# Retention outputs turned by VectorE and gated in the last stage, in a hybrid retention and MLA decode step

## The chip, the cores and the metric

The kernel runs on one core of one Trainium2 chip, as one launch. The metric is the device time of that launch in microseconds. A core has TensorE (PE, whose weight loads are shown apart as PEld), VectorE (DVE), ScalarE (ACT), GpSimd (POOL) and SyncE (SP). SP and ACT each have a queue from which they issue DMAs. All five follow their own instruction streams in order and wait for each other by semaphores.

## The reference, cut to what matters

One layer of a decoder mixes 1024 prompt tokens and 8 sequences of 4 sample tokens, 1056 columns in all. One wide projection of the normalised input gives retention queries, keys and values (4 heads, 256 for q and k, 512 for v), a SiLU gate for the retention outputs, the MLA latents and gates, and two merge gates. Retention runs over the prompt in 8 chunks of 128 tokens for each head:

```python
scores = jnp.einsum('bihd,bjhd->bhij', q, k) * dmask[None]
intra = jnp.einsum('bhij,bjhe->bihe', scores, v)
cross = jnp.einsum('bihd,bhde->bihe', q, s_prev) * q_decay[None, :, :, None]
s_new = (jnp.exp(c * log_g)[None, :, None, None] * s_prev
         + jnp.einsum('bjhd,bjhe->bhde', k * k_decay[None, :, :, None], v))
```

The retention output is normalised for each token and head over its 512 features, multiplied by a weight for each feature and by the gate, and only then projected:

```python
def retention_out(o, rg, gn_w):
    mu = jnp.mean(o, axis=-1, keepdims=True)
    var = jnp.mean(jnp.square(o - mu), axis=-1, keepdims=True)
    on = ((o - mu) * lax.rsqrt(var + EPS)).reshape(b, s, RET_VW).astype(rg.dtype)
    return on * gn_w * jax.nn.silu(rg)

h_ret = retention_out(ret_o, rg, ret_gn_w) @ w_down_ret
h_mla = (mla_o * jax.nn.silu(mg)) @ w_down_mla
merged = jax.nn.sigmoid(ga) * h_ret + jax.nn.sigmoid(gb) * h_mla
x = x + merged @ w_out
x = x + jax.nn.sigmoid(x @ w_ple_gate) * (ple @ w_ple_proj)
```

A final RMSNorm gives the outputs. All data are 32-bit floats.

## The kernel before

**Arithmetic.** Nearly every product is made of three matmuls on operands that are split into a high and a low part (`hi`, `lo`, type fp32r): `mac` (L263) multiplies high by high, high by low and low by high. The high part is a copy by ScalarE or GpSimd, the low part a subtraction by VectorE (`lo_of`, L199). `gemm` (L271) makes a 128 x 1056 output in three thirds of 352 columns, each over `nk` blocks of the inner dimension, in one of two PSUM tiles `mm`; an `evac` function takes each third out of PSUM.

**Stages in order of time.** Input turning and latents; gate projections beside the samples' attention over the paged cache, to about 730 us; retention, head by head, about 730 to 1335 us; MLA prompt attention, to about 1632 us; the MLA down projection, to about 1718 us; the retention down projection in two halves of the inner dimension, to about 1890 us; the output projection, to about 2003 us; the embedding gate and the outputs, to the end.

**Order of the work.** The program is traced as Python generators that yield costs; `woven` (L116) takes the next step of the stream that is furthest behind its share. A planner then puts the instructions of each engine in order, allots tiles from pools with a fixed number of buffers, and sets the semaphores. A DMA whose tile isn't free waits on its queue, and what stands behind it on that queue waits too.

**A retention head.** `head_qk` (L823) projects queries and keys with four gemms (q0, q1, k0, k1), each on weights that `load_w` (L254) loads and splits just ahead of it; two raw buffers `wr` and two pairs `wh`, `wl` serve all such weights. `values_of` makes the values of one chunk in `mm`. In `prompt_chunks`, `front` makes the scores of a chunk (L928), masks them (`smr`) and splits them (`smh`, `sml`); it also loads the turned keys (`knl`) that came through DRAM in `kD`. `back` multiplies scores and values into `po`, adds the product with the state, updates the state, and ends with `group_norm`, whose last instruction is ScalarE's `on` (L891). The rest of `back` is run in the next chunk's weave (`due`): `gate_out` (L899) turns `on` with four transposes on TensorE (L904), multiplies each by the feature weight `gnw` and by the gate `g` on VectorE (L908), and stores the product to `goD` (L910). `gate_in` (L894) has loaded `g` from `gtD`, where the gate projections left it, features on the partitions. Tile `g` has three buffers.

**The samples** of a head follow its chunks (`sample_state`). Their 32 tokens stand in eight rows of each group of 32 partitions of `on`; `gate_out` collects them with matmuls against a selecting matrix (L906). For all heads but the last this is put off (`late`) to the start of the next head.

**The last stages.** `gated` (L1465) loads 128 features of `goD`, already gated, for all 1056 columns; `split_gated` splits them to `gh` and `gl`. The pool `w4` has three buffers, which the gates of the merge (`gate`, L1481), the residual's tiles `xT` and two others share. In the last part `sample_rooms` (L1677) and `sample_load` (L1700) prepare the samples' share of the embedding gate: the rooms take one of 23 buffers of pool `x`, and the loads share the two `wr` buffers. They are called after the loop over the first half's four prompt tiles.

Of the kernel before, what the change touches and what calls it, by code (L numbers as in the profile page):

```python
# [162 lines left out]
def decode_step(ctx: ExitStack, tc: tile.TileContext, A: dict, O: dict):  # L163
# [29 lines left out]
    def b32(ap):  # L193
        return ap.bitcast(F32)
# [22 lines left out]
    gaD = [dram.tile([P, NT], F32, tag=f"ga{f}", name=f"ga{f}") for f in range(8)]  # L217
    gbD = [dram.tile([P, NT], F32, tag=f"gb{f}", name=f"gb{f}") for f in range(8)]
    mgD = [dram.tile([P, NT], F32, tag=f"mg{f}", name=f"mg{f}") for f in range(8)]
    gtD, goD = ([dram.tile([P, 4, NT], F32, tag=f"{n}{h}", name=f"{n}{h}") for h in range(HR)] for n in ("gt", "go"))  # L220
    latD = dram.tile([NLAT // 32, 32, SEQ], F32, tag="latD", name="latD")
    xTD = dram.tile([P, 8, NT], F32, tag="xTD", name="xTD")
    pTD = dram.tile([PLE // 32, 32, NT], F32, tag="pTD", name="pTD")
# [30 lines left out]
    def load_w(src, nk):  # L254

        hi, lo = wtiles()
        src = src.rearrange("(k p) f -> p k f", p=P)
        for k in range(0, nk, 4):
            ks = slice(k, min(k + 4, nk))
            stage(src[:, ks], hi[:, ks], lo[:, ks])  # L260
        return hi, lo
# [559 lines left out]
    kD = [dram.tile([SEQ // 32, 32, DK], F32, tag=f"kD{i}", name=f"kD{i}") for i in range(2)]  # L821

    def head_qk(h, X):  # L823
        for name, col in (("q", C_RQ), ("k", C_RK)):
            dst = X[name] = [tok(f"{name}{m}", dt=F32) for m in range(2)]

            def first(j, ps, sl, dst=dst):
                act.copy(dst[0][:, sl], ps)

            def second(j, ps, sl, dst=dst, name=name):  # L830
                x = wst.tile([P, TH], F32, tag="gev", name="rx", bufs=2)
                act.copy(x, ps)
                c, s = cosR[:, sl], sinR[:, sl]
                x0, x1 = dst[0][:, sl], dst[1][:, sl]
                t = [p4.tile([P, TH], F32, tag=f"rt{i}", name=f"rt{i}", bufs=1) for i in range(2)]
                dve.tensor_tensor(out=t[0], in0=x0, in1=s, op=ALU.mult)
                dve.tensor_tensor(out=x1, in0=x, in1=c, op=ALU.mult)
                pool.tensor_tensor(out=x1, in0=x1, in1=t[0], op=ALU.add)
                dve.tensor_tensor(out=t[1], in0=x, in1=s, op=ALU.mult)
                dve.tensor_tensor(out=x0, in0=x0, in1=c, op=ALU.mult)  # L840
                pool.tensor_tensor(out=x0, in0=x0, in1=t[1], op=ALU.subtract)
                if name == "k":
                    n = min(TH, SEQ - j * TH)
                    bs = slice(j * TH // 32, (j * TH + n) // 32)
                    for m in range(2):
                        st = p4.tile([P, TH], F32, tag=f"rt{m}", name="kb", bufs=1)[:, :n].rearrange("p (b r) -> p b r", r=32)
                        dve.transpose(st, dst[m][:, j * TH:j * TH + n].rearrange("p (b r) -> p b r", r=32))
                        for a in range(0, P, 32):
                            sp.dma_start(kD[h % 2][bs, :, m * P + a:m * P + a + 32].rearrange("b i f -> i b f"), st[a:a + 32])
            for m, evac in enumerate((first, second)):  # L850
                w = load_w(w_in[:, col + h * DK + m * P:col + h * DK + (m + 1) * P], 8)
                yield from gemm(w, xn, evac, 8)
            own = X[name + "S"] = p4.tile([P, 2, NR], F32, tag=name + "S", name=name + "S", bufs=2)
            for m in range(2):
                act.copy(own[:, m], dst[m][:, SEQ:])
# [35 lines left out]
        act.activation(on[:n], po, AF.Identity, bias=nb[:n], scale=s[:n])  # L891
        return on

    def gate_in(h, n, cols):  # L894
        g = p4.tile([P, 4, P], F32, tag="g", name="g", bufs=3)[:, :, :n]
        sp.dma_start(g, gtD[h][:, :, cols])
        return g

    def gate_out(h, on, n, cols, g):  # L899
        pt = tr()  # L900
        for f in range(4):
            o = pt[:, f * P:f * P + n]
            if n == P:
                pe.transpose(o, on[:, f * P:(f + 1) * P], ident)  # L904
            else:
                pe.matmul(o, on[:, f * P:(f + 1) * P], C("sel"), start=True, stop=True)  # L906
        for f in range(4):
            dve.scalar_tensor_tensor(out=g[:, f, :], in0=pt[:, f * P:f * P + n], scalar=gnw[:, 4 * h + f:4 * h + f + 1],  # L908
                                     in1=g[:, f, :], op0=ALU.mult, op1=ALU.mult)
        sp.dma_start(goD[h][:, :, cols], g)  # L910

    def pair(name, w, bufs, rows_=P):
        return tuple(p4.tile([rows_, w], F32R, tag=name + s, name=name + s, bufs=bufs) for s in "hl")
# [1 line left out]
    def prompt_chunks(h, X):  # L915
# [30 lines left out]
        def back(c, parts):  # L946
            sl = slice(c * P, (c + 1) * P)
            smh, sml, kh, kl = parts
            vh, vl = V.pop(c)
            if c:  # L950
                qh, ql = pair("qc", DK, 1)
                for m in range(2):
                    ms = slice(m * P, (m + 1) * P)
                    hi_pool(qh[:, ms], q[m][:, sl])
                    lo_of(ql[:, ms], q[m][:, sl], qh[:, ms])
            g = gate_in(h, P, sl)
            po = ac()
            mac(po, (smh, sml), (vh, vl), True, c == 0)
            yield 0.65
            for m in range(2 if c else 0):  # L960
                Sh, Sl = T["S"]
                ms, vs = slice(m * P, (m + 1) * P), slice(m * DV, (m + 1) * DV)
                mac(po, (qh[:, ms], ql[:, ms]), (Sh[:, vs], Sl[:, vs]), False, m == 1)
                yield 0.65
            for m in range(2):
                ms, vs = slice(m * P, (m + 1) * P), slice(m * DV, (m + 1) * DV)
                pS = ac()
                mac(pS, (kh[:, ms], kl[:, ms]), (vh, vl), True, True)
                if c:
                    dve.scalar_tensor_tensor(out=S[:, vs], in0=S[:, vs], scalar=gC, in1=pS, op0=ALU.mult, op1=ALU.add)  # L970
                else:
                    act.copy(S[:, vs], pS)
                yield 0.65
            if c < 7:
                Sh, Sl = T["S"] = tuple(p4.tile([P, 2 * DV], F32R, tag="st", name=f"St{n}", bufs=4) for n in "hl")
                for m in range(2):
                    vs = slice(m * DV, (m + 1) * DV)
                    hi_pool(Sh[:, vs], S[:, vs])
                    lo_of(Sl[:, vs], S[:, vs], Sh[:, vs])
            on = group_norm(po, P, C("qd", h, 1), C("qd2", h, 1))  # L980
            yield None
            gate_out(h, on, P, sl, g)
            yield 0.43

        def ahead(u):

# [6 lines left out]
        yield 1.0  # L993
        yield from values_of(0, X, V)
        while late:
            gate_out(*late.pop())
        due = iter(())
        for c in range(8):
            if c == 7:
                X["st"] = [states(h, 0, 0)]  # L1000
            u = back(c, parts)
            if c < 7:
                parts = front(c + 1)
                yield 1.0
                yield from woven((chain(due, ahead(u)), 3.9), (values_of(c + 1, X, V), 5.5))
                due = u
        yield None
        yield from due
# [17 lines left out]
    def sample_state(h, X):  # L1026

        q, k = X["qS"], X["kS"]
        g4 = float(np.exp(NS * lg[h]))
        sl = slice(SEQ, NT)  # L1030

        def weights(k):
            raw = p4.tile([P, DV], F32, tag="vn" + "hl"[k % 2], name="wvS", bufs=2)
# [53 lines left out]
        yield 2.0  # L1087
        px = ac()
        pe.matmul(px, sm.rearrange("p r x -> p (r x)"), vs, start=True, stop=False, skip_group_check=True)
        g = gate_in(h, NR, sl)  # L1090
        out = O["ret_sample"][0].rearrange("(r i) h (m p) e -> i m h p r e", i=2, m=2)
        turns = [(i, m) for i in range(2) for m in range(2)]
        loaded = X["st"]
# [19 lines left out]
        on = group_norm(px, P, C("qdS", h, 1), C("qd2S", h, 1))  # L1113
        yield 0.3
        if h + 1 < HR:
            late.append((h, on, NR, sl, g))
        else:
            gate_out(h, on, NR, sl, g)
            yield 0.5

    HB = 4

# [341 lines left out]

    def gated(f, pl):  # L1465
        lo = pl("gl")
        sp.dma_start(b32(lo), goD[f // 4][:, f % 4, :])
        return lo

    def split_gated(hi, lo):  # L1470

        for j in range(3):
            sl = slice(j * TH, (j + 1) * TH)
            split(b32(lo)[:, sl], hi[:, sl], lo[:, sl])
        return hi, lo

    def load_gated(f, pl):
        lo = gated(f, pl)
        return split_gated(pl("gh"), lo)

    def gate(src, f):  # L1481
        t = w4("gate", dt=F32)
# [24 lines left out]
    mph.close()  # L1507
    rph = ctx.enter_context(ExitStack())
    xr_ = slots(rph.enter_context(tc.tile_pool(name="x2", bufs=1, side="right")), "x2", 17)
    gx[7] = split_gated(xr_("gh"), gx[7])  # L1510
    merged, nxt = [], []
    for half in range(2):
        for f in range(8):
# [226 lines left out]
    for T in range(4):  # L1740
        if T < 2:
            residual(T + 2)
        proj_products(T, 0)
        joined(T, 0)
        if T < 2:
            gate_products(T + 2, 0)
        if T == 3:
            split_weight(WP, 1, 0, raw_weight("w_ple_proj", 1, 0))
        gate_weight(1, 2 * T, wtiles() if T == 3 else None)
    sp.dma_start(fnw, A["final_norm_w"].unsqueeze(0).to_broadcast([P, D]))  # L1750
    sample_rooms()
    for i in range(2):
        sample_load()
    units = [(T, 1) for T in range(4)] + [(T, H) for T in range(4, 8) for H in range(2)]
    for n, (T, H) in enumerate(units):
        if n == 1:
# [51 lines left out]
```

## Time and profile before

| | before |
|---|---|
| median of 3 runs | 2126.14 us (2125.18 to 2126.87) |
| profiled execution | 2132.47 us, span 2130.7 us |
| PE busy | 2088.9 us, 98% of the span |
| PEld, DVE, ACT, POOL busy | 1805.8, 1241.0, 698.1, 307.6 us |
| DMA | 321.91 MB in 346869 packets, mean 151 GB/s |
| ACT's DMA queue (q10) | 17280 packets, 21.63 MB |
| granted TensorE clock | 0.997 |

The span is the time between the first and the last instruction; the execution's own time is a little longer. The profiled execution is 6.3 us, 0.3%, above the median. Busy time of an engine is the union of its instructions' intervals; TensorE's matmuls overlap one another, so the distance between two starts, not a duration, says what a matmul takes. A line of the timeline has start, length, engine, line of the kernel, operation, tiles as out<-in, shape, count and, in brackets, how long the engine sat idle before it and for whom. A line of the waits has who waited for whom, the total, how often, and the longest. A row of an engine's line (L904 and so on) has the count, the shortest, median and longest duration in ns, and the first and last start in us. A queue is marked with q (ACTq, SPq): there the length is that of the issue, not of the transfer.

### The profile page before, as it was taken

The numbers are of one execution on the slowest core, as the hardware profiler recorded it, in microseconds if no ns is written. First come the engines' busy times: TensorE is split into PE (matmuls) and PEld (weight loads), VectorE is DVE, ScalarE is ACT, GpSimd is POOL, SyncE is SP. The second block draws the span as 40 slices with busy tenths as digits, with TensorE's granted clock in tenths as the row PEclk, the third lists the DMA queues.
The fourth block names the chain that finished last, engine by engine and source line by source line (L and its number), as shares of the span: only waits on it lengthen the run. The fifth ranks groups of instructions, "written<-read, shape, count | busy, mean of one in ns | idle before, by whom it ended". The sixth has DMA issues, their size and how long they took to land. (4 is left out here: it accounts for less than half of the span.)

```text
span 2130.7 us, 38543 instructions
## 1 busy us (share of the span) xinstructions
PE 2088.9 (98%) x15282; PEld 1805.8 (85%) x15282; DVE 1241.0 (58%) x2791; ACT 698.1 (33%) x1455; POOL 307.6 (14%) x517
## 2 busy tenths in 40 slices
PE   8999999999999999999999999999999999999998
PEld 7998777777777897888888887788888999999976
DVE  6524555565655356767676774877777353454433
ACT  6312232333433222322222221454556341232221
POOL 2210111111110022222222220122211000000000
PEclk9999999999999999999999999999999999999999
DMA  7586656566565432654726647210112453236642
GB/s 204 136 245 211 235 202 230 202 237 222 196 238 172 126 76 68 205 161 124 237 73 185 184 134 256 60 49 19 38 52 82 152 174 99 92 119 133 178 145 91
DMA packets 346869, 321.91 MB, mean 151 GB/s; under 512 B 126944, under 2 KB 294048, under 8 KB 342592
## 3 DMA queue, kind: packets, MB, share of 16 engines
q1 hardware_dynamic: 320192, 213.92, 34.4%
q0 software_dynamic: 9216, 83.89, 10.5%
q10 hardware_dynamic: 17280, 21.63, 2.8%
q8 instruction: 120, 1.97, 0.4%
q14 instruction: 61, 0.50, 0.1%
HBM read 246.69 MB, written 72.69 MB: 150 GB/s over the span
## 5 line engine op out<-in xcount | busy, mean ns | idle before, releaser
L267 PE MATMUL mm<-xh,wh 128*128 128x352 f32 x1344 | 456.4, 340 | 2.3 <-POOL wh L197 1.6
L269 PE MATMUL mm<-xh,wl 128*128 128x352 f32 x1344 | 436.3, 325 | 2.1 <-DVE wl L200 2.1
L268 PE MATMUL mm<-xl,wh 128*128 128x352 f32 x1344 | 436.3, 325 | 0.0
L267 PEld LDWEIGHTS mm<-xh,wh 128*128 128x128 f32 x1344 | 253.0, 188 | 86.1 <-issue 74.2
L269 PEld LDWEIGHTS mm<-xh,wl 128*128 128x128 f32 x1344 | 253.9, 189 | 4.0 <-DVE wl L200 2.4
L268 PEld LDWEIGHTS mm<-xl,wh 128*128 128x128 f32 x1344 | 254.0, 189 | 3.2 <-issue 2.1
L688 DVE STREAM_TRANSPOSE kt<-craw 128x512 f32<-128x512 f32 x256 | 161.2, 681 | 109.3 <-PE sc L692 74.8
L200 DVE TENSOR_TENSOR wl<-wr,wh 128x512 fp32r<-128x512 f32 (+2 forms) x203 | 140.1, 703 | 88.8 <-ACT wh L248 56.8
L248 ACT CAST wh<-wr 128x512 fp32r<-128x512 f32 x150 | 89.9, 617 | 203.5 <-PE mm L268 177.4
L440 ACT ACTIVATE gev<-mm 128x352 f32<-128x352 f32 x120 | 55.5, 462 | 229.4 <-PE mm L269 215.6
L267 PE MATMUL mm<-mh,wh 128*128 128x352 f32 x384 | 124.5, 324 | 1.4 <-ACT mh L1186 0.8
L268 PE MATMUL mm<-ml,wh 128*128 128x352 f32 x384 | 124.8, 325 | 0.7 <-DVE ml L200 0.6
L269 PE MATMUL mm<-mh,wl 128*128 128x352 f32 x384 | 124.3, 324 | 0.0
L269 PE MATMUL mm<-gh,wl 128*128 128x352 f32 x384 | 124.3, 324 | 0.0
L267 PE MATMUL mm<-gh,wh 128*128 128x352 f32 x384 | 124.3, 324 | 0.0
L268 PE MATMUL mm<-gl,wh 128*128 128x352 f32 x384 | 124.2, 323 | 0.0
L267 PE MATMUL mm<-wv,xh 128*128 128x512 f32 x256 | 103.5, 404 | 0.0
L268 PE MATMUL mm<-wv,xh 128*128 128x512 f32 x256 | 100.9, 394 | 0.0
L269 PE MATMUL mm<-wv,xl 128*128 128x512 f32 x256 | 100.8, 394 | 0.0
L692 PE MATMUL sc<-kt,q 32*32 32x512 f32 x2560 | 91.2, 600 | 0.0
L891 ACT ACTIVATE on<-ac,gb,gs 128x512 f32<-128x512 f32 x36 | 28.0, 778 | 157.5 <-DVE gb L889 152.4
L267 PEld LDWEIGHTS mm<-mh,wh 128*128 128x128 f32 x384 | 72.4, 188 | 1.9 <-ACT mh L1186 1.0
(419 smaller groups left out, 4370.6 us busy)
## 6 DMA issues: line engine op xcount, KB each, us to landing
wr<-in_w_in_dram SPq DMA_DIRECT2D x144, 256.0 KB
st<-in_state_ret_dram SPq DMA_DIRECT2D x32, 512.0 KB
out_ret_sample_dram<-st SPq DMA_DIRECT2D x32, 512.0 KB
gt<-gev ACTq DMA_DIRECT2D x48, 176.0 KB
gl<-go SPq DMA_DIRECT2D x16, 528.0 KB
gate<-ga SPq DMA_DIRECT2D x16, 528.0 KB
g<-gt SPq DMA_DIRECT2D x32, 256.0 KB
go<-g SPq DMA_DIRECT2D x32, 256.0 KB
```

The source lines that it names most:

```text
L200: dve.tensor_tensor(out=out, in0=src, in1=b32(hi), op=ALU.subtract)
L248: hi_by[0](hi, raw)
L267: pe.matmul(out, wh, xh, start=first, stop=False)
L268: pe.matmul(out, wh, xl, start=False, stop=False)
L269: pe.matmul(out, wl, xh, start=False, stop=last)
L440: act.activation(t, ps, func)
L688: dve.transpose(kt[:, 2 * i + s].rearrange("p (n r) -> p n r", r=32), src)
L692: pe.matmul(sc[32 * v:32 * v + 32, q, :], Q["q4"][qs_, j + v // 2, 2 * (g % 2) + v % 2, :], kt[qs_, v, :], start=n == 0, stop=n == NJ // 2 ...
L891: act.activation(on[:n], po, AF.Identity, bias=nb[:n], scale=s[:n])
```

## The change

Four things are changed.

1. The retention output of a chunk is turned by VectorE in blocks of 32 x 32 into a tile `st` (the `g` buffers), and not by TensorE. The tile is kept in a list, and in the next chunk's turn ScalarE issues four DMAs that store it to `goD`, which is now laid out as 16 blocks of 32 features; each contiguous piece of a store has 32 tokens, 128 B. The samples' `on` goes the same way, with 8 tokens a piece, and the selecting matmuls go.
2. The product with `gnw` and the gate is made in the last stages: `gated` loads 128 ungated features from `goD` and the gate from `gtD`, the latter into a buffer of `w4`, and one instruction of VectorE makes the product of 128 x 1056, which is then split.
3. In `head_qk` the weights of the next gemm are asked for at the fourth step of the gemm before. The weave's total for the chunk's own work is 3.5 in place of 3.9.
4. `sample_rooms` and the first two `sample_load` are called after the second of the four prompt tiles.

```diff
-    gtD, goD = ([dram.tile([P, 4, NT], F32, tag=f"{n}{h}", name=f"{n}{h}") for h in range(HR)] for n in ("gt", "go"))
+    gtD = [dram.tile([P, 4, NT], F32, tag=f"gt{h}", name=f"gt{h}") for h in range(HR)]
+    goD = [dram.tile([DV // 32, 32, NT], F32, tag=f"go{h}", name=f"go{h}") for h in range(HR)]
...
     def head_qk(h, X):
-        for name, col in (("q", C_RQ), ("k", C_RK)):
+        cols = [col + h * DK + m * P for col in (C_RQ, C_RK) for m in range(2)]
+        ws = []
+
+        def ask():
+            if cols:
+                col = cols.pop(0)
+                ws.append(load_w(w_in[:, col:col + P], 8))
+
+        ask()
+        for name in "qk":
...
             for m, evac in enumerate((first, second)):
-                w = load_w(w_in[:, col + h * DK + m * P:col + h * DK + (m + 1) * P], 8)
-                yield from gemm(w, xn, evac, 8)
+                for i, cost in enumerate(gemm(ws.pop(0), xn, evac, 8)):
+                    if i == 3:
+                        ask()
+                    yield cost
...
-    def gate_in(h, n, cols):
-        g = p4.tile([P, 4, P], F32, tag="g", name="g", bufs=3)[:, :, :n]
-        sp.dma_start(g, gtD[h][:, :, cols])
-        return g
-
-    def gate_out(h, on, n, cols, g):
-        pt = tr()
-        for f in range(4):
-            o = pt[:, f * P:f * P + n]
-            if n == P:
-                pe.transpose(o, on[:, f * P:(f + 1) * P], ident)
-            else:
-                pe.matmul(o, on[:, f * P:(f + 1) * P], C("sel"), start=True, stop=True)
-        for f in range(4):
-            dve.scalar_tensor_tensor(out=g[:, f, :], in0=pt[:, f * P:f * P + n], scalar=gnw[:, 4 * h + f:4 * h + f + 1],
-                                     in1=g[:, f, :], op0=ALU.mult, op1=ALU.mult)
-        sp.dma_start(goD[h][:, :, cols], g)
+    turned_out = []
+
+    def turn_out(h, on, n, t0):
+        st = p4.tile([P, DV], F32, tag="g", name="g", bufs=3).rearrange("p (b r) -> p b r", r=32)
+        dve.transpose(st, on.rearrange("p (b r) -> p b r", r=32))
+        turned_out.append((h, st, n, t0))
+
+    def store_out():
+        while turned_out:
+            h, st, n, t0 = turned_out.pop(0)
+            for a in range(4):
+                act.dma_start(goD[h][:, :, t0 + a * n:t0 + a * n + n].rearrange("b i t -> i b t"), st[32 * a:32 * a + 32, :, :n])
...
             on = group_norm(po, P, C("qd", h, 1), C("qd2", h, 1))
             yield None
-            gate_out(h, on, P, sl, g)
-            yield 0.43
+            store_out()
+            turn_out(h, on, 32, c * P)
...
-            gate_out(*late.pop())
+            turn_out(*late.pop())
...
-                yield from woven((chain(due, ahead(u)), 3.9), (values_of(c + 1, X, V), 5.5))
+                yield from woven((chain(due, ahead(u)), 3.5), (values_of(c + 1, X, V), 5.5))
...
         if h + 1 < HR:
-            late.append((h, on, NR, sl, g))
+            late.append((h, on, NS * 2, SEQ))
         else:
-            gate_out(h, on, NR, sl, g)
-            yield 0.5
+            store_out()
+            turn_out(h, on, NS * 2, SEQ)
+            store_out()
...
     def gated(f, pl):
         lo = pl("gl")
-        sp.dma_start(b32(lo), goD[f // 4][:, f % 4, :])
-        return lo
+        sp.dma_start(b32(lo), goD[f // 4][4 * (f % 4):4 * (f % 4) + 4].rearrange("b i t -> (b i) t"))
+        g = w4("rg", dt=F32)
+        sp.dma_start(g, gtD[f // 4][:, f % 4, :])
+        dve.scalar_tensor_tensor(out=g, in0=b32(lo), scalar=gnw[:, f:f + 1], in1=g, op0=ALU.mult, op1=ALU.mult)
+        return lo, g
...
-            split(b32(lo)[:, sl], hi[:, sl], lo[:, sl])
+            split(g[:, sl], hi[:, sl], lo[:, sl])
...
         gate_weight(1, 2 * T, wtiles() if T == 3 else None)
+        if T == 1:
+            sample_rooms()
+            for i in range(2):
+                sample_load()
     sp.dma_start(fnw, A["final_norm_w"].unsqueeze(0).to_broadcast([P, D]))
-    sample_rooms()
-    for i in range(2):
-        sample_load()
```

More of the change, by code (lines that the diff above doesn't have):

```diff
@@ L955, in back @@
                     lo_of(ql[:, ms], q[m][:, sl], qh[:, ms])
-            g = gate_in(h, P, sl)
             po = ac()
@@ L1029, in sample_state @@
         g4 = float(np.exp(NS * lg[h]))
-        sl = slice(SEQ, NT)
         def weights(k):
@@ L1089, in sample_state @@
         pe.matmul(px, sm.rearrange("p r x -> p (r x)"), vs, start=True, stop=False, skip_group_check=True)
-        g = gate_in(h, NR, sl)
         out = O["ret_sample"][0].rearrange("(r i) h (m p) e -> i m h p r e", i=2, m=2)
@@ L1466, in gated, with split_gated @@
         lo = pl("gl")
-        sp.dma_start(b32(lo), goD[f // 4][:, f % 4, :])
-        return lo
-    def split_gated(hi, lo):
+        sp.dma_start(b32(lo), goD[f // 4][4 * (f % 4):4 * (f % 4) + 4].rearrange("b i t -> (b i) t"))
[3 more added lines that the diff above has]
+        return lo, g
+    def split_gated(hi, lo, g):
         for j in range(3):
             sl = slice(j * TH, (j + 1) * TH)
-            split(b32(lo)[:, sl], hi[:, sl], lo[:, sl])
+            split(g[:, sl], hi[:, sl], lo[:, sl])
         return hi, lo
     def load_gated(f, pl):
-        lo = gated(f, pl)
-        return split_gated(pl("gh"), lo)
+        lo, g = gated(f, pl)
+        return split_gated(pl("gh"), lo, g)
     def gate(src, f):
@@ L1509, in decode_step @@
     xr_ = slots(rph.enter_context(tc.tile_pool(name="x2", bufs=1, side="right")), "x2", 17)
-    gx[7] = split_gated(xr_("gh"), gx[7])
+    gx[7] = split_gated(xr_("gh"), *gx[7])
     merged, nxt = [], []
```

## The prediction

> **What bounds the kernel now.** I read the page first, then the table by stretches (the retention chunks of the second head; the MLA down projection; the first half of the retention down projection and what follows), then TensorE's own waits in the retention stage.
>
> ```profile
> PE 2088.9 (98%) x15282; PEld 1805.8 (85%) x15282; DVE 1241.0 (58%) x2791; ACT 698.1 (33%) x1455; POOL 307.6 (14%) x517
> ...
> 926.00:1001.00 75.00, 75.00 (x360) 61.98 (x360) 55.93 (x144) 20.28 (x41) 20.67 (x39) 1.00 0.34 89
> 1632.00:1718.00 86.00, 86.00 (x534) 86.00 (x533) 33.08 (x61) 29.22 (x48) 2.84 (x6) 1.00 0.48 157
> 1718.00:1890.00 172.00, 172.00 (x1066) 172.00 (x1065) 84.77 (x163) 52.07 (x90) 0.00 (x0) 1.00 0.38 119
> ...
> PE ac L269 <- DVE ll L200: 1.1, 1, 1.1
> PE ac L268 <- DVE vnl L200: 1.1, 4, 0.3
> PE ac L267 <- ACT lh L1200: 1.0, 1, 1.0
> PE ac L267 <- ACT vnh L873: 0.6, 1, 0.6
> PE tr L906 <- ACT on L891: 0.4, 1, 0.4
> PE tr L904 <- ACT on L891: 0.4, 1, 0.4
> ```
>
> The columns of the middle lines are stretch, length, busy time of PE, PEld, DVE, ACT, POOL, then granted clock, DMA share and GB/s. TensorE is busy 75 of 75 us at full clock; the six last lines are all its waits between 790 and 1335 us, 4.6 us in all. So a matmul taken away here shortens the run, unless what it covered comes to light. Busy time overlaps, so I price matmuls by distances between starts, in one steady chunk:
>
> ```profile
> L904 PE MATMUL tr<-cst,on x128: 271/273/328, 801.6 to 1284.6; 128*128 128x128 f32 x128
> ...
> 970.66 0.60 PE L928 MATMUL ac<-q,k 128*128 128x128 f32 x4
> 971.10 0.60 PE L904 MATMUL tr<-cst,on 128*128 128x128 f32 x4
> 971.46 0.48 PE L267 MATMUL mm<-wv,xh 128*128 128x512 f32 x1
> ...
> 972.25 0.39 PE L267 MATMUL ac<-vnh,smh 128*128 128x512 f32 x1
> ...
> 980.60 0.60 PE L928 MATMUL ac<-q,k 128*128 128x128 f32 x4
> ...
> 969.58 0.78 ACT L891 ACTIVATE on<-ac,gb,gs 128x512 f32<-128x512 f32 x1 [6.76 <-DVE gb L889]
> 970.91 0.58 ACT L873 CAST vnh<-mm 128x512 fp32r<-128x512 f32 x1 [0.56 <-PE mm L269]
> 971.68 0.30 ACT L932 CAST smh<-smr 128x128 fp32r<-128x128 f32 x1 [0.18 <-DVE smr L931]
> ...
> 971.30 0.29 DVE L931 TENSOR_TENSOR smr<-ac,cst 128x128 f32<-128x128 f32 x1 [0.45 <-PE ac L928]
> 971.53 0.69 DVE L200 TENSOR_TENSOR vnl<-mm,vnh 128x512 fp32r<-128x512 f32 x1
> 973.34 1.12 DVE L908 SCALAR_TENSOR_TENSOR g<-tr,gnw,g 128x128 f32<-128x128 f32 x4
> ```
>
> A chunk lasts 9.94 us (970.66 to 980.60); the four transposes take 971.46 - 971.10 = 0.36 us. ACT is free for 6.76 us in each chunk ahead of `on`.
>
> **The change part by part.**
>
> *Transposes.* L904 has x128 transposes, four for each of 32 chunks: 32 x 0.36 = 11.5 us off TensorE. The samples' selecting matmuls stand below: 1327.30 - 1326.38 = 0.92 us a head. I count three heads, 2.8 us; the fourth is in the tail. With them goes the 0.4 us wait of L904 for `on`.
>
> *What comes to light.* Between the scores and the first product with `smh` TensorE now does the transposes and three value matmuls (971.10 to 972.25); `smh` is ready at 971.98, `vnl` at 972.22. Without the transposes the same order would reach that product at 971.89 and the one with `vnl` at 972.12: 0.1 us short each, one after the other rather than added, so about 0.1 us x 28 = 3 us if the order stays. In the first chunk of a head, where nothing is turned, the order already moves:
>
> ```profile
> 793.36 0.48 PE L267 MATMUL mm<-wv,xh 128*128 128x512 f32 x1
> ...
> 793.91 0.42 PE L267 MATMUL ac<-vnh,smh 128*128 128x512 f32 x1
> ...
> 794.87 0.40 PE L268 MATMUL ac<-vnl,smh 128*128 128x512 f32 x1
> ```
>
> The first product comes between value matmuls and no wait is shown. I take 1 us (0 to 3).
>
> *VectorE.* One 128x512 transpose, 0.67 us by the row below, for four multiplies, 1.12 us (973.34): 0.45 us less a chunk on an engine that is not the bound. It may start in the 0.45 us gap ahead of `smr` and delay `smr` and `vnl` by some 0.2 us; with value matmuls to fill, 0 (0 to 28 x 0.2 = 6 us).
>
> *ScalarE's stores.* Each chunk adds four DMA issues to ACT, and takes a load and a store off SP.
>
> ```profile
> L441 ACTq DMA_DIRECT2D gt<-gev x48: 326/326/327, 374.2 to 652.8; - x48
> L849 SPq DMA_DIRECT2D kD<-kb x96: 302/462/816, 783.0 to 1223.4; - x96
> L910 SPq DMA_DIRECT2D go<-g x36: 519/560/753, 805.4 to 1328.3; - x36
> L688 DVE STREAM_TRANSPOSE kt<-craw x256: 659/670/714, 187.1 to 702.4; 128x512 f32<-128x512 f32 x128
> 731.00 2.19 SPq L896 DMA_DIRECT2D g<-gt  x3
> ```
>
> ACT pays 0.33 us for an issue of 128 pieces; SP 0.46 for the `kD` stores, which have the new store's 128 B pieces, and 0.56 for 512 pieces. The new store has 32 partitions x 16 blocks = 512 pieces, so nearest is 0.56: four make 1.3 to 2.2 us, for 36 groups 47 to 81 us of ACT in a stage where it has 6.76 of 9.94 us free. In that gap it costs nothing. Ahead of `vnh` or `smh` TensorE would wait for it. The store is written a chunk late, so its data never makes ACT wait; but the order is a planner's, which asks early where it can (three `g` loads at 731 us, 60 us ahead of the first chunk), so "a chunk later" need not hold. I take 2 us, one issue in the way in a few chunks (0 to all four everywhere, in the rivals).
>
> The Trainium skill, "DMA: Bandwidth & Descriptors", section "Issuing engines are not separate DMA queues", says that the issuing sequencer's time is usually small relative to the DMA. By that the 2 us would be 0 and the time 2112; the rows above, a third to a half microsecond each, say otherwise for an engine on TensorE's path. The same page, "Specifications", asks for at least 512 B a transfer and has smaller ones read, modified and written; the new pieces have 128 B, as `kD`'s have now.
>
> *Last stage.* Sixteen multiplies of 128x1056 and sixteen more loads of 528 KB come in:
>
> ```profile
> L1666 DVE SCALAR_TENSOR_TENSOR xy<-xy,r,fnw x7: 1284/1285/1286, 2039.1 to 2110.7; 128x1024 f32<-128x1024 f32 x7
> ACT gh L1186 <- DMA gl<-go: 24.6, 11, 4.8
> DVE M L1504 <- PE mm L269: 46.9, 19, 3.4
> ```
>
> By the 1024-wide row one costs 1.3 us, 21 us in all on DVE, whose load there is 33 of 86 and 85 of 172 us (table above). The wait that ACT has for `gl` (up to 4.8 us) moves to DVE, in front of evacuations. A third of a gemm lasts about 3.9 us (DVE waits up to 3.4 us beside its 0.52), and two PSUM tiles alternate, so a delay under about 3.4 us reaches nobody. `rg` shares three buffers with the gates and its load may wait on SP for one, with the next weights queued behind it; the table shows TensorE without a gap here, so the weights have some room, which no row measures. I take 0 (0 to 16 x 1.4 = 22, were every multiply 4.8 us late).
>
> *Query and key weights.* None of TensorE's waits above names `wh` or `wl`: 0 either way.
>
> *Sample rooms earlier.* This wait should go, as the first loads then lie a few microseconds back:
>
> ```profile
> 2044.30 0.43 PE L1712 MATMUL tr<-wr,xyS 128*32 128x128 f32 x8 [0.90 <-DMA wr<-in_w_ple_gate_dram]
> 2045.00 0.43 PE L1712 MATMUL tr<-wr,xyS 128*32 128x128 f32 x8 [0.28 <-DMA wr<-in_w_ple_gate_dram]
> ```
>
> 1.2 us (0 to 1.2; a buffer fewer for raw weights could give it back).
>
> *The tail of the retention stage.*
>
> ```profile
> 1326.38 1.08 PE L906 MATMUL tr<-cst,on 128*128 128x32 f32 x8 [0.43 <-ACT on L891]
> 1327.30 0.41 PE L267 MATMUL mm<-xh,wh 128*128 128x352 f32 x1
> 1328.26 0.52 SPq L910 DMA_DIRECT2D go<-g  x1
> 1330.54 0.62 ACT L1186 CAST krA<-krT 128x512 fp32r<-128x512 f32 x1 [3.86 <-DMA go<-g]
> 1331.92 0.36 PE L267 MATMUL ac<-wqr,lh 128*128 128x256 f32 x1 [0.98 <-ACT lh L1200]
> ```
>
> The next stage waits for the last `go` store to land, 2.3 us after its issue. Now `on` must be turned (0.67) and four stores issued (1.3 to 2.2) instead of 0.92 + 0.73 of matmuls and multiplies and one issue: the landing is not earlier and perhaps 1 us later. So the last head's 0.92 us is not counted, and 1 us is added (0 to 2).
>
> **Sum.** 11.5 + 2.8 + 0.4 + 1.2 = 15.9 us off; 1 + 2 + 1 = 4 us on; net -12 us. The profiled execution took 2132.5 us (span 2130.7), 6.3 over the median 2126.1; the same difference against the median gives 2114.
>
> **Rivals.**
> 1. *ScalarE's stores get in front of `smh` (slower).* The turned tile is ready some 0.7 us after the earliest moment for `on`'s transpose, about 971.5, just as `vnh` ends and 0.18 us before `smh` starts. All four issues there hold `smh` back by 1.3 to 2.2 us, and the order shown has 0.27 us to spare (971.98 to 972.25): 1.0 to 1.9 us a chunk, over 28 chunks 28 to 53 us, so 2126 - 16 + 28 to 53 = 2138 to 2163. It decides from 0.5 us a chunk on, about one issue's length (28 x 0.5 = 14 us). For it: the gap lies there, and loads are asked early. Against: `smh` and `vnh` stand ahead of the store in the code, and the 6.76 us gap comes soon after.
> 2. *Half of that (no change).* One issue (0.33 to 0.56 us) goes first in every chunk: 9 to 16 us back: 2119 to 2128.
> 3. *VectorE waits in the last stage.* Half the bound above, 11 us back: about 2125.
> 4. *The work is covered anyway:* were the transposes filler for `smh`'s latency, only 4 us would go: 2122. Against: 24 value matmuls a chunk are there to fill.
>
> **How the numbers follow.** This measurement tells apart about 0.2%, 4.3 us. Forecast (2107 to 2121) 0.65; rival 1 0.17; rival 2 0.08; rival 3 0.05; rival 4 0.03; something slower that I don't name 0.02. The fourth and the better half of the second count as faster: 0.72; the third and the rest of the second as same: 0.09; rival 1 and the unnamed as slower: 0.19. The range: 2107 is everything gained (15.9), the waits for `vnh` and `vnl` (1.7) and 1 us for the spread of the runs (2125.2 to 2126.9); 2131 holds rivals 2 to 4 and leaves out rival 1. The likeliest case's own range is 2107 to 2121.
>
> **What would show it.** Right: no L904 and L906; 36 transposes from `on`; 144 ACT issues, and ACT's queue (q10) growing from 17280 packets by 36 x 2048 to about 91000; chunks 9.6 us apart instead of 9.94; no PE wait for `smh` or `vnh`; PE still 86 of 86 and 172 of 172 us in the last stage; the 2044 us wait gone. Wrong: PE waits named `smh`, `vnh` or `vnl` in 20 chunks or more; chunk distance at or over 9.94; DVE waits for `rg` or `gl` with PE waiting for `M` or `mev`.

## Result and profile after

The changed kernel takes 2136.6 us (median of 6 runs, 2131.9 to 2138.1) against 2125.7 us (2123.6 to 2127.1) for the kernel before on the same chip: ratio 1.0046, 95% interval 1.0035 to 1.0058, some 10 us slower. The forecast was 2114 (2107 to 2131), 12 us faster. The profiled execution took 2135.1 us, span 2133.4. In the profiles below the time up to the first scores varies between 777 and 792 us, whatever the edit, so stages are compared from there on.

First the page of the changed kernel: the engines, ACT's queue (packets, MB, share), and the stores (count, KB each, us to landing).

```profile
PE 2085.1 (98%) x15122; PEld 1791.9 (84%) x15122; DVE 1229.5 (58%) x2699; ACT 696.5 (33%) x1455; POOL 308.5 (14%) x517
...
q10 hardware_dynamic: 93312, 30.29, 5.4%
...
go<-g ACTq DMA_DIRECT2D x128, 64.0 KB, 1.9
```

The matmuls are gone (15122 in place of 15282) and the stores are there. Yet TensorE's busy time fell by only 3.8 us: part of it now runs at half clock, as shown below. TensorE's waits in the retention stage (total, times, longest), changed kernel:

```profile
PE ac L269 <- DVE vnl L200: 9.0, 9, 2.5
PE ac L1070 <- DMA wvS<-in_w_in_dram: 2.7, 3, 2.2
PE ac L268 <- ACT vnh L885: 0.4, 1, 0.4
```

Before, the waits for `vnl` were 1.1 us in all and at most 0.3. Three of the nine are 2.4 to 2.5 us, in the second chunk of heads 1, 2 and 3 (heads are counted from 0); the long one for `wvS`, the value weights of the samples' part, is in the last head. Stretches of the changed kernel (length, busy PE, PEld, DVE, ACT, POOL, then granted clock, DMA share, GB/s):

```profile
927.50:929.90 2.40, 0.02 (x1) 0.02 (x1) 1.82 (x5) 0.64 (x2) 0.55 (x1) 1.00 0.11 19
931.10:934.50 3.40, 3.40 (x9) 2.67 (x8) 1.91 (x7) 1.36 (x2) 1.17 (x2) 0.50 0.50 90
1071.10:1074.50 3.40, 3.40 (x10) 2.62 (x9) 1.58 (x6) 1.26 (x2) 1.17 (x2) 0.50 0.48 79
1211.00:1214.40 3.40, 3.40 (x10) 2.63 (x9) 2.03 (x7) 1.36 (x2) 1.17 (x2) 0.50 0.54 99
1296.30:1303.10 6.80, 6.70 (x45) 3.86 (x44) 1.39 (x2) 1.49 (x3) 0.00 (x0) 0.50 0.89 265
1632.00:1718.00 86.00, 84.49 (x522) 83.83 (x521) 42.06 (x69) 27.15 (x47) 3.01 (x6) 1.00 0.57 190
1718.00:1890.00 172.00, 171.69 (x1062) 171.43 (x1061) 95.11 (x170) 53.57 (x91) 0.00 (x0) 1.00 0.47 148
```

Right behind each of the four long waits the clock stands at 0.50 for 3.4 or 6.8 us: 17 us at half speed, 8.5 us lost. The kernel before has no such stretch between its first scores and 1330 us; it has one of 3.4 us at 1334 us, which the changed kernel has not. The last two rows are the last stages, nearly full as before; they lie some 5 us later here, so the first of them still holds the end of MLA.

The loss is in the retention stage: from the first scores to the first matmul of MLA it takes 554.5 us in place of 545.2. TensorE is idle for 14.9 of them (3.5 before) and busy for 539.7 (541.6 before), of which 8.5 are lost to the half clock. By distances between scores, the three second chunks are 13.7 us longer and the end of the last head 3.8; the later chunks of all four heads are 5.4 us shorter and the first ones 2.5.

How the long wait comes about shows in the second head's start. ScalarE, VectorE and TensorE of the changed kernel:

```profile
906.64 0.62 ACT L249 CAST wh<-wr 128x512 fp32r<-128x512 f32 x1 [3.05 <-DMA wr<-in_w_in_dram]
...
911.97 0.62 ACT L249 CAST wh<-wr 128x512 fp32r<-128x512 f32 x1 [4.36 <-DMA wr<-in_w_in_dram]
912.49 0.45 ACT L842 COPY rx<-mm 128x352 f32<-128x352 f32 x1
...
921.67 0.78 ACT L903 ACTIVATE on<-ac,gb,gs 128x512 f32<-128x512 f32 x1 [5.80 <-DVE gb L901]
923.23 0.89 ACTq L917 DMA_DIRECT2D go<-g  x2
924.21 0.45 ACT L842 COPY rx<-mm 128x352 f32<-128x352 f32 x1 [1.76 <-DVE k L850]
...
922.48 0.71 DVE L910 STREAM_TRANSPOSE g<-on 128x512 f32<-128x512 f32 x1 [0.85 <-ACT on L903]
...
924.70 0.65 DVE L847 TENSOR_TENSOR k<-rx,cosR 128x352 f32<-128x352 f32 x1 [0.34 <-ACT rx L842]
...
928.08 0.97 DVE L857 STREAM_TRANSPOSE kb<-k 128x352 f32<-128x352 f32 x2 [1.04 <-POOL k L851]
928.98 0.25 DVE L938 TENSOR_TENSOR smr<-ac,cst 128x128 f32<-128x128 f32 x1
929.15 0.67 DVE L200 TENSOR_TENSOR vnl<-mm,vnh 128x512 fp32r<-128x512 f32 x1
...
926.98 0.39 PE L268 MATMUL mm<-wv,xh 128*128 128x512 f32 x1
929.88 0.50 PE L269 MATMUL ac<-vnl,smh 128*128 128x512 f32 x1 [2.51 <-DVE vnl L200]
```

The same place in the kernel before:

```profile
911.60 0.62 ACT L248 CAST wh<-wr 128x512 fp32r<-128x512 f32 x1
...
925.37 0.78 ACT L891 ACTIVATE on<-ac,gb,gs 128x512 f32<-128x512 f32 x1 [2.97 <-DVE gb L889]
926.05 0.44 ACT L832 COPY rx<-mm 128x352 f32<-128x352 f32 x1
...
929.99 0.97 DVE L847 STREAM_TRANSPOSE kb<-k 128x352 f32<-128x352 f32 x2 [1.06 <-POOL k L841]
...
933.17 0.68 DVE L200 TENSOR_TENSOR vnl<-mm,vnh 128x512 fp32r<-128x512 f32 x1
```

`rx` is the copy out of PSUM from which the rope of the keys reads. Before, the last one follows `on` at once, 0.46 us after the head's first scores (925.59), and the key turns `kb` are done 2.2 us ahead of `vnl`. Two weight casts stand ahead of the rope's first `rx` in both kernels. Before, the second has its load in time (911.60); now they wait 3.05 and 4.36 us for their loads, with that `rx` behind them. The group norm is late with it: `on` starts 2.61 us after the first scores (919.06), where before it started 0.22 us ahead of them. Then `on`, its turn and two stores stand in front of the last `rx`, which comes 5.15 us after the first scores. (The bracket there names `k`, but in heads 1, 2 and 3 that `rx` starts 0.09 to 0.10 us after the second issue ends, and the bracket of head 3 names `smr`.) VectorE takes its instructions in order: the rope's steps wait for that `rx` at 924.70, `kb` for the rope at 928.08, and `vnl`, whose input `vnh` was ready at 926.36, stands behind them all. Head 2 looks the same. In head 3 the second cast waits 3.20 us, `on` starts 1.24 us after the scores and the last `rx` 4.03.

### The profile page after: what moved, and what is told of

It reads as the page before. It is cut to its first block, busy times and chain, and to the rows that moved or that the text cites. A ratio compares the mean times of both kernels' runs of the same rounds, so it can differ in the third digit from the quotient of the medians.

```text
span 2133.4 us, 38257 instructions
## 1 busy us (share of the span) xinstructions
PE 2085.1 (98%) x15122; PEld 1791.9 (84%) x15122; DVE 1229.5 (58%) x2699; ACT 696.5 (33%) x1455; POOL 308.5 (14%) x517
## 3 DMA queue, kind: packets, MB, share of 16 engines
q10 hardware_dynamic: 93312, 30.29, 5.4%
## 5 line engine op out<-in xcount | busy, mean ns | idle before, releaser
L200 DVE TENSOR_TENSOR wl<-wr,wh 128x512 fp32r<-128x512 f32 (+2 forms) x203 | 135.1, 678 | 119.2 <-ACT wh L249 90.0
```

Source lines behind the costliest of these rows:

```text
L200: dve.tensor_tensor(out=out, in0=src, in1=b32(hi), op=ALU.subtract)
```

## Experiments

Each kernel is compared with the kernel before on the same chip; "us" is the ratio times 2126, less 2126. "Second chunk" is the distance from the second to the third scores in heads 1, 2, 3; "chunks 3 to 7" the sum of the next five distances over these heads; "stage" runs from the first scores to the first matmul of MLA. All three are from the profiles. The weave's total of 3.5 in place of 3.9 was not tested by itself.

| kernel | ratio to before (95%) | us | second chunk | chunks 3 to 7 | stage |
|---|---|---|---|---|---|
| before | 1 | 0 | 8.2, 8.2, 8.2 | 149.1 | 545.2 |
| changed | 1.0046 (1.0035 to 1.0058) | +10 | 12.7, 12.8, 12.7 | 146.1 | 554.5 |
| e1 no early asking | 0.9992 (0.9983 to 1.0001) | -2 | 8.2, 8.2, 9.4 | 147.5 | 547.2 |
| e2 stores by SP | 1.0053 (1.0040 to 1.0066) | +11 | 10.3, 9.8, 10.1 | 145.2 | 555.4 |
| e3 both | 1.0104 (1.0089 to 1.0119) | +22 | 8.6, 10.2, 9.5 | 145.1 | 569.6 |
| e4 before, early asking alone | 0.9986 (0.9978 to 0.9995) | -3 | 8.2, 8.2, 8.2 | 149.1 | 543.8 |
| e5 turns behind vnl | 0.9949 (0.9935 to 0.9962) | -11 | 9.4, 8.2, 11.8 | 143.3 | 536.7 |
| e6 e1 and e5 | 0.9961 (0.9948 to 0.9974) | -8 | 8.2, 8.2, 8.2 | 143.3 | 535.1 |
| e7 latents late | 1.0025 (1.0012 to 1.0038) | +5 | 11.2, 11.2, 13.7 | 146.0 | 550.1 |
| e8 e5 and e7 | 0.9947 (0.9935 to 0.9960) | -11 | 9.8, 8.2, 8.6 | 143.4 | 535.5 |
| e9 stores behind vnh | 1.0005 (0.9995 to 1.0015) | +1 | 12.1, 9.8, 12.2 | 146.5 | 545.2 |
| e10 e5, stores twice | 1.0128 (1.0113 to 1.0143) | +27 | 9.7, 9.6, 10.2 | 148.2 | 572.2 |
| e11 e5, first cast held | 0.9993 (0.9982 to 1.0003) | -1 | 8.2, 8.2, 11.9 | 143.3 | 551.8 |
| e12 e5, no gating | 0.9952 (0.9936 to 0.9968) | -10 | 9.4, 8.2, 8.8 | 143.3 | 534.6 |
| e13 steady turns alone | 0.9964 (0.9950 to 0.9978) | -8 | 10.9, 9.9, 9.3 | 143.3 | 539.4 |
| e14 samples' turns alone | 0.9963 (0.9949 to 0.9978) | -8 | 9.7, 9.7, 9.8 | 145.9 | 539.4 |
| e15 changed again | 1.0035 (1.0023 to 1.0047) | +7 | 12.7, 13.9, 13.5 | 146.1 | 558.6 |

### Is it the stores or the early asking? (e1 to e4)

```diff
# e1, e3: head_qk as before, weights loaded ahead of their own gemm
# e4: the kernel before with the new head_qk
# e2, e3:
-                act.dma_start(goD[h]...
+                sp.dma_start(goD[h]...
```

> The changed kernel with each query or key weight loaded just ahead of its own gemm again; everything else as changed. Theory B (asking early): the next head's weights are cast by ScalarE in front of the rope's copies, the rope is late, and the value split of the second chunk waits behind it. Then TensorE's three waits for vnl in the second chunk of heads 1 to 3 (2.7, 2.7 and 2.5 us) go, and with them the three stretches at half clock behind them (3.4 us each, 1.7 us lost each): 13 us off 2136.6, about 2124. Theory A (ScalarE's stores hold up the rope): the three waits stay, 2135 to 2138.

> The changed kernel with the retention stores issued by SP and not by ScalarE. Theory A: the three waits for vnl and their half-clock stretches go (13 us), and the wait for wvS at 1295 us with its 6.8 us at half clock too (2.3 + 3.4 us): 2118 to 2124. Theory B: the four stores take about 1 us ahead of the rope's copy, so each wait shrinks by no more than that, from 2.6 to about 1.6 us: 2131 to 2136. If SP's loads of keys or weights come late behind the stores, new waits for knh or wr show up and the time is above 2137.

> Both edits: weights loaded as before, stores issued by SP. If either cause alone makes the three waits, this is no better than the better of the two single edits; if each makes a part of them, it is 3 us or more faster than both. Theory A: 2118 to 2122, as the stores on SP alone. Theory B: 2119 to 2124, the waits gone through the weights and the last head's 5.7 us perhaps through the stores.

> The kernel before with only the weights asked for a tile ahead, nothing else changed. Theory B: waits for vnl or smh in the second chunk of heads 1 to 3 show up here too, 1 to 4.4 us a head with the half clock: 2129 to 2139. Theory A: no such waits, 2125 to 2127. The rival to both, that it takes the two edits together (the stores and the early casts in one order): this one 2125 to 2127 and each of the single edits near 2124.

Without the early asking the second chunk is back at 8.2 us in two of three heads; the weight cast of head 1 has its load in time again (908.63, no wait). But asking early in the kernel before gives no wait for `vnl` at all and gains 3 us. So neither theory holds by itself: the long waits need the early asking together with what the change put behind `on`. With SP's stores the second chunk falls by 2.7 us a head, and the gain is lost again: SP's other transfers come late. Both edits together are worse than either, which no expectation had: there TensorE waits 4.7 and 4.6 us for `wh` and `wl`, whose loads SP issues too. TensorE's longest waits with stores by SP, retention stage:

```profile
PE ac L269 <- DVE vnl L200: 7.7, 8, 1.9
PE ac L268 <- DMA wr<-in_w_uq_dram: 5.2, 1, 5.2
PE tr L1081 <- ACT vs L1078: 4.0, 3, 1.5
```

### The turn in front of vnl (e5, e6), the last head's loads (e7, e8)

Steady chunks of the changed kernel were 9.46 to 10.05 us apart, where the forecast had 9.94 - 0.36 = 9.58 throughout. VectorE and TensorE in one of them, changed kernel:

```profile
957.57 0.71 DVE L910 STREAM_TRANSPOSE g<-on 128x512 f32<-128x512 f32 x1
958.20 0.25 DVE L938 TENSOR_TENSOR smr<-ac,cst 128x128 f32<-128x128 f32 x1
958.38 0.67 DVE L200 TENSOR_TENSOR vnl<-mm,vnh 128x512 fp32r<-128x512 f32 x1
...
958.55 0.40 PE L268 MATMUL mm<-wv,xh 128*128 128x512 f32 x1
959.11 0.50 PE L269 MATMUL ac<-vnl,smh 128*128 128x512 f32 x1 [0.16 <-DVE vnl L200]
```

The planner puts the turn right ahead of `smr` and `vnl`; the product with `vnl` starts 0.56 us after its neighbour and not 0.23. e5 adds one edge to the order (no wait; the lines that keep hold of the latest `vnl` are left out here):

```diff
-        dve.transpose(st, on.rearrange("p (b r) -> p b r", r=32))
+        with tc.issue_after(split_of["v"].ins):     # the latest vnl on VectorE
+            dve.transpose(st, on.rearrange("p (b r) -> p b r", r=32))
# e6: the same on e1
# e7, e8: the loads from latD traced after 28 steps of the last head's gates,
#         pinned behind the loads of wvS on SP
```

> The changed kernel with one order edge: VectorE's turn of an output is queued behind the value split vnl that TensorE wants next, so that the turn, and the stores that wait for it, no longer stand in front of the rope's copy at a head's start. The early weight casts stay there. Theory C (it takes the stores and the early casts together, as the first four runs say): the second chunk of heads 1 to 3 loses the stores' share of its wait, about 1 to 1.5 of 2.6 us, and the half clock if the wait falls below what sets it off (3.4 us at half clock, 1.7 lost): 8 to 10 us for three heads. Theory D (turns ahead of vnl cost each steady chunk 0.1 to 0.4 us): chunk distances of 9.58 to 9.62 in place of 9.6 to 10.0, 3 us. Both: 2124 to 2128. If the casts alone keep the rope late: 2133 to 2136.

> The same order edge on the kernel without the early asking (its steady chunks were 9.8 to 10.05 us apart). Theory D: the small waits for vnl go, chunks 9.58 to 9.65 us apart, 24 x 0.25 = 6 us off 2125.6: 2119 to 2121. If the chunks stay at 9.8 or over, the waits come from ScalarE's vnh behind a store and not from the turn: 2124 to 2127.

> The changed kernel with the seven loads of the latents and rotary keys (latD) issued on SP behind the last head's value weights wvS, not ahead of them; the rest as changed. Theory E (the 128 B pieces of the stores share a saturated DMA with these loads at 1268 to 1284 us, both issuing queues stand still, on comes 6.9 us late and wvS 2.2 us): the wait for wvS at 1295 us and its 6.8 us at half clock go, 4 to 6 us: 2131 to 2133. Against it: wvS is late on SP by its own buffers, and the time stays at 2135 to 2138.

> Both edits, the turn behind vnl and the latents late. If the causes are separate the gains add: 2119 to 2124, below the kernel before. If the last head's wait only moves (the latents are then late for the next stage's lh at 1335 us), the time is that of the order edge alone.

The edge turns +10 us into -11, better than the expected -2 to +2. A steady chunk in e5, VectorE and TensorE:

```profile
969.12 0.29 DVE L939 TENSOR_TENSOR smr<-ac,cst 128x128 f32<-128x128 f32 x1 [0.35 <-PE ac L936]
...
970.12 0.68 DVE L200 TENSOR_TENSOR vnl<-mm,vnh 128x512 fp32r<-128x512 f32 x1
...
971.31 0.70 DVE L911 STREAM_TRANSPOSE g<-on 128x512 f32<-128x512 f32 x1
...
968.48 0.60 PE L936 MATMUL ac<-q,k 128*128 128x128 f32 x4
...
971.46 0.39 PE L269 MATMUL ac<-vnl,smh 128*128 128x512 f32 x1
...
977.94 0.60 PE L936 MATMUL ac<-q,k 128*128 128x128 f32 x4
```

Here `vnl` is done at 970.80, the product starts at 971.46 without a wait, and the chunks are 9.46 us apart. What is left in the second chunks goes with the casts: in heads 1 and 3, where the second cast waits 4.18 and 4.15 us for its load and the rope's first `rx` comes 6.9 and 6.7 us ahead of the first scores, they take 9.4 and 11.8 us; in head 2, with 3.08 us of wait and `rx` 8.7 us ahead (9.2 in the kernel before), 8.2. Once the turns are out of the way, the early asking is worth nothing either way (e6 and e5 overlap).

The theory of the saturated DMA in the last head falls: with the latents late the wait for `wvS` is 2.4 us (2.2 in the changed kernel), and e8 is no faster than e5. e7 is nearer to the kernel before than the changed one, though its interval overlaps that of the changed kernel; fewer stretches at half clock behind its second chunks go with that. After a wait of 2.50 us for `vnl` the first of these rows of e7 has the full clock; the second, after 2.35 us in the last head, has half:

```profile
935.40:938.80 3.40, 3.40 (x15) 2.79 (x16) 2.45 (x8) 0.84 (x2) 1.19 (x2) 1.00 0.56 93
1213.30:1216.70 3.40, 3.40 (x9) 2.65 (x9) 1.77 (x6) 0.46 (x1) 0.55 (x1) 0.50 0.53 88
```

### Prices of the parts (e9 to e12)

```diff
# e9, on the changed kernel: the stores (not the turns) behind the latest vnh
+            with tc.issue_after(split_of["v"].ins):     # here ScalarE's vnh
                 for a in range(4):
                     act.dma_start(goD[h]...
# e10, on e5: every store also into a second tensor
# e11, on e5: the casts of a head's first query weights behind vnh and vnl
# e12, on e5: gated() leaves out the gate's load and the product
```

> The changed kernel with only ScalarE's stores queued behind the next vnh; VectorE's turn stays in front of vnl, the early casts stay. Against the kernel before the changed one was +11 us, the one with the turn behind vnl -11 us. Theory A2 (most of it is the stores in front of the rope's copy and in the sample part): the second chunks of heads 1 to 3 shrink as there, from 12.7 to about 9 us, steady chunks stay at 9.6 to 10.0: -8 to -4 us against before. Theory D2 (most of it is the turn in front of vnl on VectorE): the second chunks stay at 11 to 12.7 us and the time at +5 to +11 us.

> The kernel with the turn behind vnl, and every store issued a second time into a second tensor: 288 issues in place of 144, 16.4 + 16.4 MB... of 128 B pieces in all twice as many. If issues that stand behind vnl are hidden in ScalarE's free 6.8 us of a chunk, as the prediction had it, the time stays within 2 us of that kernel, -12 to -9 us against before. If each issue costs on the path (0.33 us or more) or the pieces slow the other transfers: 4 x 0.33 x 28 = 37 us, or waits for wvS, st or knl show up; -5 us or worse.

> The kernel with the turn behind vnl, and the casts of the next head's first query weights held behind the first chunk's vnh and vnl. If those casts, in front of the rope's copies, are what is left of the second chunk's wait (9.4, 8.2 and 11.8 us in heads 1 to 3), the three are 8.2 us and the time falls by 3 to 5 us: -16 to -13 us against before. If the wait comes from the rope itself, no change: -12 to -9 us.

> The kernel with the turn behind vnl, without the product with the gate and the feature weight in the last stages and without the gate's loads; this part of the result is left out. It prices the last stage's new work. The prediction had 0 (0 to 22 us). If VectorE and the loads there are covered: -13 to -10 us against before. If the product makes evacuations late beyond the one wait seen at 1700 us: -15 us or better.

e9 lies between: with the stores out of the way some two fifths of the gap to e5 are closed, with the turns too the rest. Of the 9.3 us by which its stage is shorter than the changed kernel's, 4.2 are in the second chunks and 4.7 in the end of the last head, where the 6.8 us at half clock are gone. The gating is free: without it the time is that of e5. TensorE's waits in the retention stage with the stores doubled (e10), then with the first cast held (e11):

```profile
PE ac L1072 <- DMA wvS<-in_w_in_dram: 15.4, 17, 2.8
PE ac L268 <- ACT vnh L885: 8.4, 5, 5.4
```

```profile
PE ac L1074 <- DMA wvS<-in_w_in_dram: 6.3, 6, 1.8
PE tr L1060 <- POOL ks L1057: 3.7, 6, 1.0
```

e10: of the five steady distances of a head, eight issues leave the third and the fourth as they were with four (9.47 us). The Trainium skill, "DMA: Bandwidth & Descriptors", section "Issuing engines are not separate DMA queues", calls the sequencer's time for an issue usually small relative to the DMA; these two distances fit that. The first (10.7 us in place of 9.6, with a wait of TensorE of 0.93 us for `vnh` in head 1) and the last (9.94 in place of 9.47) do not: 4.9 us over three heads. In the samples' part (from the eighth chunk's scores to the next head's first) it takes 78 to 80 us in place of 72, 20 us over three heads, and the end of the last head 10 us more; together these are most of the 38 us that e10 loses against e5. (One set of stores is 8.7 MB in the page of ACT's queue, not the 16.4 of the expectation.) Some 27 us of e10's stage are at half clock (3.4 in e5), so that 12 us of the loss are the clock's. So the four issues and their pieces have a price, which these runs don't split. e11 shows that the casts are what keeps the rope late (8.2 us in the two heads whose casts it holds; the last head has no next query weights and stays at 11.9), and that holding them costs more: the samples' part takes 76 to 79 us. That the held casts keep the raw buffers `wr` from the next loads is argued, not shown.

### Which turns? (e13 to e15)

```diff
# e13: the edge only for turns with t0 < SEQ;  e14: only for t0 == SEQ;  e15: no edge
```

> The changed kernel with only the turns of the prompt's chunks queued behind vnl; the samples' turn at a head's start, and its stores in front of the rope's copy, stay. If the steady chunks carry the loss: 9.47 us apart as with all turns moved, second chunks still 11 to 12.7 us, 5 to 8 us below the changed kernel. If the head's start carries it: 1 to 4 us below.

> The reverse: only the samples' turn at a head's start queued behind vnl, with it the stores out of the way of the rope's copy; the steady turns stay in front. If the head's start carries the loss: second chunks at 8.2 to 10.5 us, steady ones at 9.6 to 10.0, 8 to 13 us below the changed kernel. If the steady chunks carry it: second chunks stay over 11 us, 1 to 4 us below. The two runs together should make some 15 to 20 us.

> The changed kernel, unaltered, on the chip of the other two: 0.4 to 0.6% above the kernel before if the ratio holds from chip to chip.

Each half of the edge alone brings 15 us on one chip (1.0035 to 0.9964 and 0.9963), so the halves don't add; both beat their expectations. From e15 to e13 the three second chunks lose 10.1 us, though the samples' turn stays where it was: TensorE's idle time in them shrinks from 8.4 to 4.8 us, and the 13.6 us at half clock behind them (6.8 us lost) are gone. The steady chunks give 2.8 us there, and 0.2 us in e14, as it should be. The rest is in the last head, whose wait for `wvS` (4.3 us in e15, 2.2 in e13, none in e14) comes and goes with the order; why was not settled, nor why the second chunks of e13 gain by an edge on other turns.

## Why the prediction was wrong, point by point

- *Transposes, selecting matmuls: 14.3 us off.* The size was right. With the turns out of the way (e5) the five steady distances are 0.39 us less than before on average ((149.1 - 143.3) / 15), and 0.47 in the last three, against 0.36 forecast; the samples' matmuls show as 0.82 us a head (0.92 forecast) in the distance of the first two scores, 7.06 to 6.24, in all versions of the changed kernel. That e5 comes out at -11, near the forecast of -12, is in part luck: its second chunks are still 4.9 us longer than before, which the sum had not.
- *VectorE: 0 (0 to 6). This step failed.* It named the right gap, the one ahead of `smr`, and 0.2 us of delay to `vnl` a chunk, and then took 0 because value matmuls would fill. In the steady chunks the delay was 0.19 us ((146.1 - 143.3) / 15), 5 us over 28: inside the range. What the range had not was the head's start, where the turn stands in a chain of `on`, stores, `rx`, rope and `kb`, all ahead of `vnl`: 2.4 to 2.5 us of waiting in each of three heads, and the half clock behind it.
- *ScalarE's stores: 2 us, rival 1 from 0.5 us a chunk.* The premise that their data never makes ScalarE wait, which the prediction itself doubted, failed at the head's start: there the issues begin 0.04 us after the turn ends (923.19), with `rx` behind them. Rival 1 had the right sign and the wrong victim: no wait for `smh`, nine for `vnl` and not twenty; that its 2138 lies so near the result is luck. (Rival 2's range, by its own sum, would be 2121 to 2128.) e9 takes back 6 to 9 us (from 1.0035 or 1.0046 to 1.0005), not quite half of it in the second chunks, where the stores stood in front of `rx`.
- *Query and key weights: 0, since no wait named `wh` or `wl`. This failed too.* What an early request delays does not bear its name: the two casts ahead of the rope's first `rx` wait 3.05 and 4.36 us for their loads, and TensorE's wait that follows is for `vnl`. Alone it is harmless (e4), with the turns in front it makes 9 to 11 us (the changed kernel's two ratios against e1). Which loads ahead of them on SP made these late was not followed.
- *Nothing in the sum had the clock.* 8.5 us of the changed kernel's retention stage (10.2 in e15) are that.
- *Last stage: 0.* Right. VectorE now waits 32.7 us for `gl`, and TensorE once. Its waits from 1632 us on that have to do with the change, changed kernel and then the kernel before:

```profile
PE mm L268 <- ACT gh L1191: 0.9, 1, 0.9
```

```profile
PE tr L1712 <- DMA wr<-in_w_ple_gate_dram: 1.2, 2, 0.9
```

- *Sample rooms: 1.2.* Right: that wait is gone.
- *Tail: +1 (0 to 2).* Right: the wait for `lh` at the start of MLA grew from 1.0 to 1.6 us. The last head's wait for `wvS`, 2.2 us, was not seen.
- *Signs.* 144 issues and 93312 packets (about 91000 forecast) came as said; the chunk distance of 9.6 us was met in single chunks only.

## What to carry to other kernels

Work that is moved to an engine off the critical path must be placed, not only priced: ask which instruction in that engine's order the bounding engine waits for next, and put the new work behind it with an order edge; here one edge on the turn was worth 18 to 21 us. A change that asks for data earlier can delay an instruction that never names that data, so follow every engine's order at the seams between stages, not in the steady loop alone. Version e5 (ratio 0.9949), with or without e7's edit, beats both kernels.

## What the hardware showed

A wait of TensorE of 2.2 to 2.5 us can cost two thirds as much again or more: the granted clock then stands at 0.50 for 3.4 us (1.7 us lost) or a multiple (6.8 us after 1296 us), and matmuls start 0.42 us apart in place of 0.23 (931.14 to 931.56). At that length it comes or stays away: all three waits for `vnl` in the changed kernel's second chunks set it off, one of three like them in e7, and e13 went through 2.46 us without it. A wait of 1.83 us did it in e5, three of up to 1.4 us in e14 did not. The Trainium skill, "TensorE: Matmul & The Clock Gate", section "What's actually happening", has half rate after an idle window of about 3.4 us and a window that runs freely. The length of the stretches agrees; here waits well below 3.4 us were enough. That it depends on where a wait falls in such a window would fit, but no run here shows it.
